# Where the scaling of the final norm's weights stands on ScalarE in the last feed-forward group

## The chip, the cores and the metric

The kernel runs on one NeuronCore of a Trainium2 chip. The metric is the device time of one execution in microseconds (us), as the median of several runs. All inputs lie in the chip's memory (HBM) at the start, and the output is written back there. Engines are called PE (TensorE matmuls), PEld (TensorE weight loads), DVE (VectorE), ACT (ScalarE), POOL (GpSimd) and SP (SyncE, which here only issues DMAs).

## What is computed

A trunk of two layers over 512 tokens of width 1024 in float32. Each layer has two groups of attention heads that share a projection, and then a dense feed-forward part with a squared ReLU. A final RMS norm with its own weights `final_norm` closes the trunk.

```python
def rmsnorm(x, g):
    return x * lax.rsqrt(jnp.mean(x * x, axis=-1, keepdims=True) + EPS) * g

for l in range(DEPTH):                                   # DEPTH = 2
    h = rmsnorm(x, attn_norm[l])
    ...                                                  # two kinds of attention, one output projection
    x = x + jnp.einsum('bse,ed->bsd', mixed, w_o[l])
    h = rmsnorm(x, mlp_norm[l])
    u = jnp.square(jax.nn.relu(jnp.einsum('bsd,df->bsf', h, w_ff1[l])))   # 1024 -> 4096
    x = x + jnp.einsum('bsf,fd->bsd', u, w_ff2[l])                        # 4096 -> 1024
return rmsnorm(x, final_norm)
```

## The kernel before

**Products in three matmuls.** Every float32 operand is split in a rounded part and a rest: for weights `whi` (rounded on ACT, L115) and `wlo` (the difference, made on DVE, L131). Each product is three matmuls (`three`, L297 with hi·hi, L298 with `wlo`, L299 with the activation's rest `Al`), which accumulate in one PSUM bank. Four pairs of buffers hold the split weights of the feed-forward part, used in turn: the rounding of a new tile waits until PE has done the last matmul with the tile four places earlier.

**Feed-forward groups.** The 4096 hidden columns are worked on in four groups (`GROUPS`). A group first makes its activations (`quad_group`, chains X, V, Y over `h`), and splits them into seven forms `Ah`, `Al` (L237 on ACT, L238 on DVE; the squared ReLUs stand in L1045 and L1046, sums of forms in L945). Then it multiplies the forms by seven sums of quarters of `w_ff2`, in the order `FORMS2`: "11", "x3", "21", "x2", "x1", "x4", "22". Each form has two weight tiles (called 0 and 1 below: x3/0, x3/1 and so on), and each tile serves twelve matmuls of 512 columns. The forms accumulate in three chains of two PSUM banks each: 11, x2, x1, 22 in X; x3, x4 in V; 21 in Y.

**Gathers.** After a form, `gather` (L1084) reads its two banks on DVE, scales them by the row factors and adds them to the result tiles `y`. Form x1 goes on accumulating in X, so its matmuls wait until the gather of x2 has read the banks.

**Weight sums by DMA.** `grow` (L861, L863) loads a quarter of `w_ff2` with SP or adds one to a tile in place with a POOL DMA. The adding load for x2 is issued as soon as the split of x3 has read the tile (x2/0 after x3/0, x2/1 after x3/1).

**End of the last group of the last layer.** Two DMAs of SP (L1245), written down after form x3, fetch `gfin` (the final norm's weights, to all 128 partitions) into `gf[0]` and `gf[1]`, which are pieces of `x`; they wait on SP for the last readers of these pieces. At form x2 three ACT instructions make the scaled weights: `gf[0]` by the root of D, `gf[1]` by minus that (L1247, L1248 of the profile), and `x[:, 0, 0:256]` from half of `gf[1]` (L1249). After form x1, four squares (`square`, L1107 on ACT) begin the sums for the last norm, and four `weigh` (L1145 on DVE) multiply finished pieces of `y` by `gf`. Form "22" and a chain of squares, roots (POOL, L1140), scalings and stores end the kernel.

**Order.** The program is written as one sequence; a scheduler that runs when the kernel is built, with a cost model of its own, places the instructions on each engine's queue by their dependencies and the order they were written in. An engine runs its queue strictly in that order. `behind(a, b)` adds an edge without a semaphore: `a` is placed after `b`. `in_order(a, b, c, ...)` chains such edges. `W.last[0]` is the newest rounding on ACT that has been written down when the line is reached; `W.do_split` writes them four tiles ahead of their use, so at form x2 the newest one is that of x4/0.

Of the kernel before, what the change touches and what calls it, by code (L numbers as in the profile page):

```python
# [12 lines left out]
AF = mybir.ActivationFunctionType  # L13
# [6 lines left out]
D = 1024  # L20
# [143 lines left out]
def trunk(ctx, tc, opened, xT, w, w2, w1, gfin, lamv, cos, sin, out):  # L164
    nc = tc.nc
# [19 lines left out]
    W = _Weights(nc, w, wraw, wspl)  # L185
# [3 lines left out]
    x = cp.tile([P, KC, S], F32, tag="x", name="x")  # L189
# [42 lines left out]
    r2 = cp.tile([P, 4], F32, tag="r2", name="r2")  # L232
# [27 lines left out]
    def behind(a, b):  # L260
        tc.add_manual_dep(a.ins, b.ins.name, mybir.DependencyInfo(
            mybir.DependencyClass.NoSync, mybir.DependencyReason.DATA), reason="order")
# [44 lines left out]
    def block(name, tag="mm"):  # L307
        pt = bank(tag, name)
        u = W.next("px" if name[0] == "p" else "1")
        for c in range(KC):  # L310
            three(pt, wpair(u, c), hpair(c), c == 0, c == KC - 1)
            yield pt if c == KC - 1 else None
# [20 lines left out]
    for l in range(L):  # L333
# [502 lines left out]
        with ExitStack() as fctx:  # L836
# [223 lines left out]
            def rest_of_forms(j, form):  # L1060
                F = [chunk(j, k) for k in range(4)]
                hi, lo = ([e[:, k, :, :].rearrange("p a t -> p (a t)") for k in range(7)] for e in sides[j])
                if form == "21":
                    split(hi[2], lo[2], F[3])
                elif form == "x2":
                    split_less(hi[5], lo[5], F[2])
                elif form == "22":
                    tt2(F[3], F[2], F[3], ALU.subtract)
                    split(hi[6], lo[6], F[3])
# [3 lines left out]
            def place(tb, j):  # L1073
                return y[(tb // 2, j)][:, tb % 2, :]
# [15 lines left out]
            def forth(tb, j):  # L1090
                pt = bank("t", f"xT{tb}{j}")
                for k in range(4):
                    nc.tensor.transpose(pt[:, k * P : (k + 1) * P], x[:, 4 * j + k, tb * P : (tb + 1) * P], ident)
                nc.scalar.activation(place(tb, j), pt, AF.Copy, scale=-1.0 if j else 1.0)
# [63 lines left out]
            def in_order(*steps):  # L1158
                for p, q in zip(steps[1:], steps):
                    behind(p, q)  # L1160

            gf = [x[:, 2, :], x[:, 3, :]]
# [5 lines left out]
            for g in range(GROUPS):  # L1168
                end = g == GROUPS - 1
                turn[0] = 0  # L1170
                if g:
                    p_, q_, r_, s_ = r_, s_, p_, q_
                    quad_group(g, 0, (p_, q_, r_))
                    quad_group(g, 1, (s_, r_, q_))
                    rest_of_forms(1, "21")
                else:
                    for k in range(2 * GP):
                        for n, pt in enumerate(block(f"f{l}_{g}_{k}", "any")):
                            if (k, n) == (1, 0):
                                rms_square(ssq, f"m{l}")  # L1180
                        evict_whole(pt, k)
                        h_form(k)
                        if last and k > 3:
                            for tb in (2 * (k % 2), 2 * (k % 2) + 1):
                                forth(tb, 1 - k // 6)
                    p_, q_, r_, s_ = ring[0] % 3, 3, (ring[0] + 1) % 3, (ring[0] + 2) % 3
                    held_on = {"Y": [bank("t", f"Y{l}{r}") for r in range(2)], "V": [bank("mm", f"V{l}{r}") for r in range(2)]}
                chains = {"X": [temp(k, f"X{l}{g}{k}") for k in (p_, q_)], **held_on}
                for form in FORMS2:
                    total, to = SUMS[form], chains[CHAIN[form]]  # L1190
                    opens = form == "11" or g == 0 and form in ("x3", "21")
                    if form == "x4" and not end:
                        to = [temp(k, f"W{l}{g}{k}") for k in (r_, s_)]
                        opens = True
                    work = [(c, i, r, 0) for c in range(GP // 2) for i in range(2) for r in range(2)]
                    tail = end and form == "22"
                    if tail and last:
                        gather(total, to)
                        to = [temp(k, f"Z{l}{k}") for k in (r_, s_)]
                        opens = True  # L1200
                        work = [(c, i, r, n) for r, n in ((0, 0), (1, 1), (1, 2)) for c in range(GP // 2) for i in range(2)]
                        halves = [to[1], bank("mm", "half")]
                        nc.tensor.matmul(
                            halves[1][:, 0:256], zeros[:, 0:128], zeros[:, 128:384], start=True, stop=False)
                        seed = nc.scalar.activation(
                            halves[1][:, 0:256], place(3, 1)[:, 256:512], AF.Copy, scale=mean[:, 3:4])
                    elif end and last and form == "x4":
                        work.sort(key=lambda e: e[2])
                    held = {}
                    for n, (c, i, r, part) in enumerate(work):  # L1210
                        if c not in held:
                            held[c] = W.next("f")
                        u = held[c]
                        hi, lo = (e[:, :, i, :] for e in sides[c])
                        rs = slice(r * P, r * P + P)
                        mine = [m for m, e in enumerate(work) if e[2:] == (r, part)]
                        pt, b_ = to[r], wpair(u, i, 512)
                        if part:
                            pt = halves[part - 1][:, 0:256]
                            b_ = [e[:, 256 * part - 256 : 256 * part] for e in b_]  # L1220
                        three(pt, (hi[:, SIDE[form], rs], lo[:, SIDE[form], rs]), b_,
                              opens and n == mine[0] and part < 2, n == mine[-1], not opens)
                        if tail and last and n == 3:
                            squares.append(square(0, 0))
                            first += [root(0), store(0, 0, False), came[1]]
                            squares += [seed, store(0, 1, True), square(1, 0)]
                            first += [root(1), store(1, 0, False), *gather(total, to, (0,))]
                            squares += [store(1, 1, True), square(2, 1)]
                            first.append(root(2))
                        if end and not last and form == "22" and n % 2:  # L1230
                            h = back(n // 2)
                            rests.append(h[1])
                            halfway = h
                    if tail:
                        break
                    if end or form not in ("x3", "21"):
                        came = gather(total, to)
                    if g and form in ("11", "x3"):
                        rest_of_forms(1, "x2" if form == "11" else "22")
                    if end and not last and form in ("21", "x2"):  # L1240
                        for c in range(4 * (form == "x2"), 4 * (form == "x2") + 4):
                            nc.sync.dma_start(x[:, c, :], park[c])
                    if end and last and form == "x3":
                        for c in range(2):
                            nc.sync.dma_start(gf[c], gfin[512 * c : 512 * c + 512].partition_broadcast(P))  # L1245
                    if end and last and form == "x2":
                        nc.scalar.activation(gf[0], gf[0], AF.Copy, scale=math.sqrt(D))  # L1247
                        nc.scalar.activation(gf[1], gf[1], AF.Copy, scale=-math.sqrt(D))  # L1248
                        nc.scalar.activation(x[:, 0, 0:256], gf[1][:, 256:512], AF.Copy, scale=r2[:, 3:4])  # L1249
                    if end and last and form == "x1":  # L1250
                        done = ((2, 0), (3, 0), (0, 1), (1, 1))
                        squares = [square(*e) for e in done]
                        weighed = [weigh(*e) for e in done]
                    elif end and last and form == "x4":
                        first = [came[0]]
# [94 lines left out]
```

## Time and profile before

| | us |
|---|---|
| median of 3 runs | 1139.09 |
| the runs | 1136.55, 1139.55, 1139.09 |
| profiled execution | 1138.57 |
| its span, first to last instruction | 1136.5 |
| PE busy in the span | 1122.4 (99%) |
| DVE busy | 914.9 (81%) |
| ACT busy | 687.0 (60%) |

The profiled execution takes 2.07 us outside its span. Times in the timeline are counted from the start of the span. In the timeline a row gives the start, the time an instruction takes, the engine, the line, out<-in with shapes, how many such instructions follow each other directly, and in brackets how long the engine had idled before it and what ended that idle time. The columns of the table by stretches of time stand in the order of the engines PE, PEld, DVE, ACT, POOL, then PEclk (granted TensorE clock, 1 is full), the busy share of the DMA engines, and GB/s. Matmuls are pipelined: one takes 0.39 us from start to end, and the next starts well before that.

### The profile page before, as it was taken

To read this page: it belongs to the slowest core of one execution; us is meant where nothing else is said; L and a number is where in the kernel's file an instruction comes from. 1 tells how busy PE (TensorE), PEld (TensorE's weight loads), DVE (VectorE), ACT (ScalarE), POOL (GpSimd) and SP (SyncE) were. 2 spreads that over 40 slices of the span, in tenths; PEclk is the share of its full clock that TensorE was granted. 3 is DMA by queue.
4 is the path that set the end of the run, shared out by engine and by line. 5 is a ranking of instruction groups with operands and counts; after the bars stand their busy time and mean duration, and the time that the engine had idled before them with its cause. 6 is when DMAs were issued, how large, how long until landed. Compare 5 with 4: busy or idle time off the path is not lost.

```text
span 1136.5 us, 17656 instructions
## 1 busy us (share of the span) xinstructions
PE 1122.4 (99%) x6613; PEld 992.6 (87%) x6613; DVE 914.9 (81%) x1329; ACT 687.0 (60%) x1115; POOL 137.5 (12%) x221
## 2 busy tenths in 40 slices
PE   9999999999999999999999999999999999999996
PEld 7899889888899899898888998988888998988975
DVE  7898788788669879779788877887877797797886
ACT  6456666567558457476345565675774574764763
POOL 1001343101001001001000014330010010010000
PEclk9999999999999999999999999999999999999998
DMA  7665353266877657738227544512487577567261
GB/s 250 149 187 147 93 168 112 74 207 161 234 195 165 173 163 168 204 110 224 75 78 206 162 131 130 159 65 75 167 198 199 159 167 204 149 154 216 78 128 75
DMA packets 59317, 174.99 MB, mean 154 GB/s; under 512 B 7264, under 2 KB 8544, under 8 KB 59232
## 3 DMA queue, kind: packets, MB, share of 16 engines
q1 hardware_dynamic: 50160, 141.84, 39.9%
q0 software_dynamic: 8640, 31.46, 15.8%
q8 instruction: 52, 0.85, 0.3%
q10 hardware_dynamic: 432, 0.56, 0.1%
q14 instruction: 33, 0.27, 0.1%
HBM read 144.47 MB, written 4.19 MB: 131 GB/s over the span
## 4 chain that ended last, share of the span: by engine, by line
PE 88%; DVE 5%; DMA 2%; issue 2%; ACT 1%; SPq 1%; POOL 0%; POOLq 0%; DVEq 0%; ACTq 0%
PE X L297 8%; PE X L298 8%; PE X L299 8%; PE V L297 3%; PE V L298 3%; PE V L299 3%; PE wo L297 3%; PE wo L299 3%; PE wo L298 3%; PE f L297 3%; PE f L299 3%; PE f L298 3%; PE Y L298 2%; PE Y L297 2%; PE Y L299 2%
## 5 line engine op out<-in xcount | busy, mean ns | idle before, releaser
L115 ACT ACTIVATE whi<-q 128x1024 fp32r<-128x1024 f32 x96 | 101.3, 1058 | 105.8 <-PE X L299 36.7
L131 DVE TENSOR_TENSOR wlo<-q,whi 128x1024 fp32r<-128x1024 f32 x96 | 116.9, 1221 | 42.2 <-ACT whi L115 39.1
L115 ACT ACTIVATE whi<-raw 128x1024 fp32r<-128x1024 f32 (+1 forms) x82 | 80.7, 992 | 49.6 <-issue 20.3
L131 DVE TENSOR_TENSOR wlo<-raw,whi 128x1024 fp32r<-128x1024 f32 (+1 forms) x82 | 95.2, 1168 | 10.9 <-ACT whi L115 10.5
L297 PE MATMUL X<-whi,Ah 128*128 128x512 f32 x248 | 98.2, 396 | 0.0
L298 PE MATMUL X<-wlo,Ah 128*128 128x512 f32 x248 | 97.1, 392 | 0.0
L299 PE MATMUL X<-whi,Al 128*128 128x512 f32 x248 | 96.9, 391 | 0.0
L131 DVE TENSOR_TENSOR wlo<-waves,whi 128x1024 fp32r<-128x1024 f32 x40 | 48.9, 1222 | 17.0 <-ACT whi L115 16.8
L115 ACT ACTIVATE whi<-waves 128x1024 fp32r<-128x1024 f32 x40 | 42.2, 1055 | 29.9 <-PE X L299 14.8
L297 PEld LDWEIGHTS X<-whi,Ah 128*128 128x128 f32 x248 | 46.9, 189 | 12.1 <-DVE y L1084 1.9
L299 PEld LDWEIGHTS X<-whi,Al 128*128 128x128 f32 x248 | 46.9, 189 | 10.0
L297 PE MATMUL X<-hxh,whi 128*128 128x256 f32 x192 | 54.9, 286 | 0.4 <-DVE x L1041 0.2
L298 PEld LDWEIGHTS X<-wlo,Ah 128*128 128x128 f32 x248 | 46.9, 189 | 9.0
L299 PE MATMUL X<-h_hi,wlo 128*128 128x256 f32 x192 | 54.4, 283 | 0.0
L298 PE MATMUL X<-h_lo,whi 128*128 128x256 f32 x192 | 54.4, 283 | 0.0
L298 PE MATMUL X<-hxl,whi 128*128 128x256 f32 x192 | 54.3, 283 | 0.0
L299 PE MATMUL X<-hxh,wlo 128*128 128x256 f32 x192 | 54.3, 283 | 0.0
L297 PE MATMUL X<-h_hi,whi 128*128 128x256 f32 x192 | 54.3, 283 | 0.0
L297 PE MATMUL f<-h_hi,whi 128*128 128x512 f32 x128 | 50.3, 393 | 0.0
L863 POOL DMA_DIRECT2D q<-in_w x32 | 28.7, 898 | 177.9 <-DVE wlo L131 177.9
L299 PE MATMUL f<-h_hi,wlo 128*128 128x512 f32 x128 | 49.9, 390 | 0.0
L298 PE MATMUL f<-h_lo,whi 128*128 128x512 f32 x128 | 49.8, 389 | 0.0
(740 smaller groups left out, 3819.1 us busy)
## 6 DMA issues: line engine op xcount, KB each, us to landing
raw<-in_w SPq DMA_DIRECT2D x78, 512.0 KB, 3.8
q<-in_w SPq DMA_DIRECT2D x48, 512.0 KB, 4.7
q<-in_w POOLq DMA_DIRECT2D x48, 512.0 KB, 7.5
waves<-in_w SPq DMA_DIRECT2D x28, 512.0 KB, 4.7
first_a<-in_w SPq DMA_DIRECT2D x12, 512.0 KB, 4.9
first_b<-in_w SPq DMA_DIRECT2D x12, 512.0 KB, 5.1
first_c<-in_w SPq DMA_DIRECT2D x12, 512.0 KB, 3.7
norms<-in_w SPq DMA_DIRECT2D x12, 512.0 KB, 3.6
```

Of the source, the lines that this page charges most:

```text
L115: return self.nc.scalar.activation(o, src, AF.Copy)
L131: self.last = h, nc.vector.tensor_tensor(out=lo[:, a:b], in0=raw[:, a:b], in1=hi[:, a:b].bitcast(F32), op=ALU.subtract)
L297: nc.tensor.matmul(pt, ah, bh, start=first, stop=False, skip_group_check=goes_on)
L298: nc.tensor.matmul(pt, ah, bl, start=False, stop=False, skip_group_check=goes_on)
L299: nc.tensor.matmul(pt, al, bh, start=False, stop=last, skip_group_check=goes_on)
L863: nc.gpsimd.dma_start(t, quad(g, q, c), accum_op=ALU.add)
```

## The change

The three ACT instructions that scale the final norm's weights are chained behind each other and behind the newest weight rounding on ACT.

```diff
                     if end and last and form == "x2":
-                        nc.scalar.activation(gf[0], gf[0], AF.Copy, scale=math.sqrt(D))
-                        nc.scalar.activation(gf[1], gf[1], AF.Copy, scale=-math.sqrt(D))
-                        nc.scalar.activation(x[:, 0, 0:256], gf[1][:, 256:512], AF.Copy, scale=r2[:, 3:4])
+                        in_order(
+                            W.last[0], nc.scalar.activation(gf[0], gf[0], AF.Copy, scale=math.sqrt(D)),
+                            nc.scalar.activation(gf[1], gf[1], AF.Copy, scale=-math.sqrt(D)),
+                            nc.scalar.activation(x[:, 0, 0:256], gf[1][:, 256:512], AF.Copy, scale=r2[:, 3:4]))
```

Later lines move down by one (L1247 to L1249 become L1248 to L1250). The queue of ACT, as the two programs were built, differs in this stretch; roundings are named by their weight tile, the right column is after the change:

```
before                               after
rounding x3/0                        rounding x3/0
L1045 relu                           L1045 relu
L1248 scale gf[1]                    L1046 square
L1046 square                         rounding x3/1
L1055 relu                           L237
L237                                 L1055 relu
L1056 square                         L237 (1024 columns)
L237 (1024 columns)                  L1056 square
L237                                 rounding 21/0
rounding x3/1                        L237
rounding 21/0                        L242
L242                                 rounding 21/1
rounding 21/1                        rounding x2/0
L1247 scale gf[0]                    rounding x2/1
rounding x2/0                        rounding x1/0
rounding x2/1                        L237
rounding x1/0                        rounding x1/1
L237                                 L1107 square
L1249 scale x[:, 0, 0:256]           rounding x4/0
rounding x1/1                        L1248 scale gf[0]
rounding x4/0                        L1249 scale gf[1]
L1107 square, twice                  L1107 square
rounding x4/1                        L1250 scale x[:, 0, 0:256]
rounding 22/0                        rounding x4/1
                                     rounding 22/0
```

On DVE the same instructions stand in the stretch: the split of x3/1 (`wlo`) moves forward by four places, that of 21/0 by one, and one `weigh` moves ahead of the split of x4/1. On PE one matmul of form x4 (L298) moves from ahead of the matmuls of x1 to behind them, and the matmul that prepares the last bank (L1203) moves ahead by one. The queues of POOL and SP keep their order.

## The prediction

> **What bounds the kernel now.** I read the page first, for the busy shares.
>
> ```profile
> PE 1122.4 (99%) x6613; PEld 992.6 (87%) x6613; DVE 914.9 (81%) x1329; ACT 687.0 (60%) x1115; POOL 137.5 (12%) x221
> ```
>
> PE sets the pace, so the change can gain only where PE stands still, or in the tail behind it. The edit touches a few microseconds in the last group. So the second view is the timeline of ACT there, with two rows of the preceding half group for comparison.
>
> ```profile
> 1062.37 1.06 ACT L1045 ACTIVATE x<-x 128x1024 f32<-128x1024 f32 x1 [0.95 <-DVE x L945]
> 1063.46 1.06 ACT L1046 ACTIVATE x<-x 128x1024 f32<-128x1024 f32 x1
> ...
> 1081.96 1.04 ACT L1045 ACTIVATE x<-x 128x1024 f32<-128x1024 f32 x1
> 1085.81 0.63 ACT L1248 ACTIVATE x<-x 128x512 f32<-128x512 f32 x1 [2.81 <-DMA x<-in_gfin]
> 1086.35 1.04 ACT L1046 ACTIVATE x<-x 128x1024 f32<-128x1024 f32 x1
> ```
>
> The scaling L1248 got between the ReLU and the square. It waits 2.81 us for the DMA of `gfin`, and the square L1046 waits behind it. In the half group before, L1046 starts 1.09 us after L1045, here 4.39 us. Who waits for the square is seen on DVE.
>
> ```profile
> 1082.09 1.23 DVE L131 TENSOR_TENSOR wlo<-q,whi 128x1024 fp32r<-128x1024 f32 x1 [0.28 <-ACT whi L115]
> 1087.42 1.42 DVE L945 TENSOR_TENSOR x<-x 128x512 f32<-128x512 f32 x2 [4.11 <-ACT x L1046]
> ...
> 1105.34 1.41 DVE L1084 SCALAR_TENSOR_TENSOR y<-Y,r,y 128x512 f32<-128x512 f32 x2
> 1106.66 2.36 DVE L131 TENSOR_TENSOR wlo<-q,whi 128x1024 fp32r<-128x1024 f32 x2
> 1108.93 1.41 DVE L1084 SCALAR_TENSOR_TENSOR y<-X,r,y 128x512 f32<-128x512 f32 x2
> ```
>
> DVE idles 4.11 us, and then never catches up, as the table by stretches shows: from 1087.42 to 1109.02, where the second `wlo` of the row at 1106.66 (that of x4/0) ends, it is busy for 21.53 of 21.60 us (third column).
>
> ```profile
> 1087.42:1109.02 21.60, 19.08 (x83) 15.13 (x81) 21.53 (x26) 15.26 (x22) 0.86 (x1) 1.00 0.48 109
> ```
>
> PE pays for that twice.
>
> ```profile
> 1091.98 0.39 PE L297 MATMUL V<-whi,Ah 128*128 128x512 f32 x1
> 1093.10 0.50 PE L298 MATMUL V<-wlo,Ah 128*128 128x512 f32 x1 [0.73 <-DVE wlo L131]
> 1093.44 0.39 PE L299 MATMUL V<-whi,Al 128*128 128x512 f32 x1
> ...
> 1106.61 0.61 PE L297 MATMUL V<-whi,Ah 128*128 128x512 f32 x2
> 1109.08 0.53 PE L298 MATMUL V<-wlo,Ah 128*128 128x512 f32 x1 [1.85 <-DVE wlo L131]
> 1109.42 0.61 PE L299 MATMUL V<-whi,Al 128*128 128x512 f32 x1
> ...
> 1112.82 0.40 PE L299 MATMUL X<-whi,Al 128*128 128x512 f32 x1
> 1113.06 0.39 PE L297 MATMUL X<-whi,Ah 128*128 128x512 f32 x1
> ...
> 1116.91 0.39 PE L299 MATMUL X<-whi,Al 128*128 128x512 f32 x1
> ```
>
> The first wait is for the `wlo` of x3/1, the second for that of x4/0. The granted clock (third value from the end) falls right after the second:
>
> ```profile
> 1105.00:1110.00 5.00, 3.15 (x13) 2.28 (x12) 5.00 (x7) 2.54 (x6) 0.00 (x0) 0.94 0.35 105
> 1110.00:1115.00 5.00, 5.00 (x18) 3.97 (x17) 2.68 (x4) 0.33 (x1) 0.00 (x0) 0.72 0.01 3
> 1115.00:1120.00 5.00, 5.00 (x24) 4.14 (x23) 4.24 (x5) 3.01 (x6) 0.00 (x0) 1.00 0.01 2
> ```
>
> Last, what the end hangs on: the rounding of 22/0 on ACT, and DVE behind it.
>
> ```profile
> 1114.67 1.06 ACT L115 ACTIVATE whi<-q 128x1024 fp32r<-128x1024 f32 x1 [6.21 <-issue]
> 1115.76 1.23 DVE L131 TENSOR_TENSOR wlo<-q,whi 128x1024 fp32r<-128x1024 f32 x1 [3.08 <-ACT whi L115]
> 1115.76:1122.60 6.84, 6.84 (x32) 5.50 (x31) 6.84 (x9) 2.83 (x7) 0.00 (x0) 1.00 0.00 0
> ```
>
> That rounding takes the buffers of x1/0, and so waits for the twelfth matmul of form x1 (second of the rows below, 1114.19 plus 0.39 is 1114.58). Behind it DVE works without a gap, and then DVE, ACT and POOL hand each other squares and roots to the end. So the end moves by as much as this twelfth matmul does.
>
> ```profile
> 1110.68 0.63 PE L297 MATMUL X<-whi,Ah 128*128 128x512 f32 x1
> 1114.19 0.39 PE L299 MATMUL X<-whi,Al 128*128 128x512 f32 x1
> ```
>
> **The change, part by part.** The pace of PE at full clock is 3.85 us for the 17 steps from 1113.06 to 1116.91, 0.2265 us each.
>
> *The square moves forward.* With no scaling ahead of it, L1046 starts 1.09 us after L1045, at 1083.05 instead of 1086.35: 3.30 us earlier. L945 starts 1.07 us behind the square, as now, so DVE takes up its work at 1084.12.
>
> *DVE keeps most of that lead.* Up to the `wlo` of x4/0 it has the same 26 instructions in another order, 21.60 us: that `wlo` would end at 1105.72 instead of 1109.02. What could hold DVE in between is PE or ACT. Y, the chain gathered before it, ends 72 steps after the group's first matmul (1083.80, below), at 1100.1, its gather comes at 1102.0. ACT's roundings wait for PE to free buffers, as now, and come before DVE needs them. I take the lead at x4/0 as 2.9 to 3.3 us, because ACT and DVE wait for each other in small pieces (0.35 us at one L237 below, and 0.07 in the next step).
>
> *The new wait.* x4/0's rounding now stands behind a square L1107, which waits for the first Y gather. That gather ends at 1105.34 + 0.75 − 3.30 = 1102.79, half of the 1.41 us row with the overlap. The square with its read takes 0.66 us (1106.13 to 1106.79), the rounding 1.04: 1104.5 to 1104.6. DVE reaches the split at 1105.72 − 1.23 = 1104.49. It costs at most 0.1. Behind the rounding now stand three scalings (0.63, 0.62 and 0.49 us below), another square and the rounding of x4/1. That tile is needed behind the 24 matmuls of x1, over 5 us later, so these cost nothing; without this cover they would cost their 1.7 us.
>
> ```profile
> 1083.80 0.40 PE L297 MATMUL X<-whi,Ah 128*128 128x512 f32 x1
> 1093.73 0.62 ACT L1247 ACTIVATE x<-x 128x512 f32<-128x512 f32 x1
> 1101.46 0.63 ACT L237 ACTIVATE Ah<-x 128x512 fp32r<-128x512 f32 x1 [0.35 <-DVE x L945]
> 1102.00 0.49 ACT L1249 ACTIVATE x<-x,r 128x256 f32<-128x256 f32 x1
> 1106.13 0.63 ACT L1107 ACTIVATE x<-y 128x512 f32<-128x512 f32 x1 [0.92 <-DVE y L1084]
> 1106.79 0.63 ACT L1107 ACTIVATE x<-y 128x512 f32<-128x512 f32 x1
> ```
>
> *PE's first wait goes.* The split of x3/1 moves ahead of four DVE instructions, and DVE is early. The rows show 1.12 and 0.34 us for two steps of 0.23: 1.00 us back.
>
> *PE's second wait goes, nearly.* From 1106.61 to the third matmul it takes 2.47 us instead of two steps (0.45), and then 0.34 for 0.23: 2.13 us back. PE, 1.00 earlier, wants the `wlo` of x4/0 at 1106.06. DVE has it at 1109.08 − 3.30 = 1105.78; PE stalls when DVE's lead falls below 3.02. With a lead of 2.9 it would stall 0.1. The gather of x2 then runs beside the other V matmuls; x1 needs it after five of these instead of six, so up to 0.2 more. I take 0.35 for the two, bounds 0 and 0.8 (a lead of 2.5, twice the small waits).
>
> *The slow clock goes with it.* From 1109.42 to 1112.82 eight steps take 3.40 us instead of 1.81: 1.59 us back. The idle time left, 0.1 to 0.4 us, is less than the 0.73 at 1093.10, after which the steps ran at full pace.
>
> *One V matmul moves behind x1*: 0.23 us sooner for the twelfth matmul of x1.
>
> Sum: 1.00 + 2.13 + 1.59 + 0.23 − 0.35 = 4.60 us. The profiled execution took 1138.57, so 1133.97, rounded **1134.0 us**. It lies 0.5 below the median of the three runs, which spread by 3.0; that spread goes into the range.
>
> A rule speaks against one term. The Trainium skill, page "TensorE: Matmul & The Clock Gate", section "Why this matters for your kernels", says that gaps of over some 3 us between bursts of matmuls bring the half clock, one window of idleness. The trace differs: 1.85 us were followed by it.
>
> **The rivals.**
>
> *The slow clock has another cause than this gap.* For: one case is thin evidence. Against: it begins 0.3 us after the gap. Then 1.59 stays: 1138.57 − 3.01 = 1135.6 us. By the skill's rule just named, this would be the outcome.
>
> *DVE's lead melts.* If ACT's new order (the rounding of x4/0 behind a square behind a gather) costs 1.2 us more than worked out, PE stalls for over 1 us there, and the slow clock comes again. Then the first wait, 1.00, the moved matmul, 0.23, and some 0.6 of the second are gained: 1136.7 us. For: DVE is busy to 99.7% there, and has only 0.28 us to spare. Against: the instructions are the same.
>
> *It does nothing to DVE*, because the square waits for something else: 1138.6 us. Against it: L1045 ended at 1083.0, and the square of the preceding half group followed its ReLU at once.
>
> *Slower: the adding load of x2/1 collides.* It is issued when the split of x3/1 has read the tile, and so moves from 1093.40 to about 1086.6, from an idle stretch of the DMA engines into a full one (1.04 and 0.16 in the rows).
>
> ```profile
> 1083.67 0.86 POOL L863 DMA_DIRECT2D q<-in_w x1 [1.88 <-DVE wlo L131]
> 1093.40 0.86 POOL L863 DMA_DIRECT2D q<-in_w x1 [8.87 <-DVE wlo L131]
> 1085.00:1090.00 5.00, 5.00 (x24) 4.14 (x23) 2.51 (x4) 4.19 (x7) 0.00 (x0) 1.00 1.04 230
> 1090.00:1095.00 5.00, 4.27 (x19) 3.23 (x18) 5.00 (x7) 5.00 (x7) 0.86 (x1) 1.00 0.16 28
> 1099.10 2.01 ACT L115 ACTIVATE whi<-q 128x1024 fp32r<-128x1024 f32 x2 [3.81 <-DVE y L1084]
> ```
>
> Now it takes 5.7 us until the rounding of x2/1 starts (1093.40 to 1099.10). Started only when the others are through, near 1091, it would be there at 1096.7; DVE wants the split at 1098.0, a rounding (1.06) before that is 1096.9. Past this point each us delays DVE, the Y gather, the square and x4/0 by one. Landing at 1105 would cost 8 us, make 1134.0 into 1142 us and bring the slow clock anyway. Against: the queue would have to stand for 8 us.
>
> **How the numbers follow.** Forecast, 1134.0: 0.70; its own range is 1132.0 (no residual stall, and runs 1.6 lower) to 1135.8. Slow clock stays, 1135.6: 0.09. Lead melts, 1136.7: 0.11. Nothing, 1138.6: 0.04. Slower, 1142: 0.06. The range 1132.0 to 1137.0 takes in the first three. A change of 0.3%, 3.4 us, is about what a measurement of this kernel can tell from none. Faster by more: the forecast and a little of the others, 0.73. Within: 0.21. Slower: 0.06.
>
> **What would show it.** In the changed profile L1046 follows L1045 by 1.1 us, DVE's idle time at L945 is below 1 us, both waits of PE for `wlo` in V are gone or below 0.4 us, the clock is 1.00 up to the tail, and the rounding of 22/0 starts near 1110. A wait of DVE for the rounding of x2/1 or x4/0 of over 0.5 us, or a clock below 1 between 1100 and 1115, would make the forecast wrong.

## The result, and the profile after

| | kernel before | changed kernel |
|---|---|---|
| median, runs side by side | 1138.67 us (6 runs, 1136.55 to 1140.04) | 1133.62 us (6 runs, 1132.63 to 1134.12) |
| profiled execution | 1138.57 us, span 1136.5 | 1134.11 us, span 1132.2 |
| first matmul of the last half group (the forms' products with `w_ff2`, from form "11" on) to the end of the span | 1136.5 − 1083.80 = 52.70 us | 1132.2 − 1084.47 = 47.73 us |

The ratio is 0.9957, with a 95% interval of 0.9944 to 0.9970: 5.05 us faster in the medians; 1134.0 us had been forecast. The third line of the table is used throughout below. The profiled executions of this kernel and its variants reach the last half group anywhere between 1082.25 and 1087.09 us, and this spread comes about ahead of the edit. Counted from that half group's first matmul (1083.80 before, 1084.47 after), only the stretch in which the edit acts is compared.

ACT around the ReLU (L1045) and the square (L1046), and then around the three scalings at their new place (L1248 to L1250, one line further down than before), in the timeline of the changed kernel:

```profile
1082.63 1.04 ACT L1045 ACTIVATE x<-x 128x1024 f32<-128x1024 f32 x1
1083.71 1.06 ACT L1046 ACTIVATE x<-x 128x1024 f32<-128x1024 f32 x1
...
1103.57 0.63 ACT L1107 ACTIVATE x<-y 128x512 f32<-128x512 f32 x1 [1.44 <-DVE y L1084]
1104.20 1.04 ACT L115 ACTIVATE whi<-q 128x1024 fp32r<-128x1024 f32 x1
1105.15 0.61 ACT L1248 ACTIVATE x<-x 128x512 f32<-128x512 f32 x1
1105.67 0.61 ACT L1249 ACTIVATE x<-x 128x512 f32<-128x512 f32 x1
...
1110.37 1.06 ACT L115 ACTIVATE whi<-q 128x1024 fp32r<-128x1024 f32 x1 [2.12 <-PE X L299]
```

The square follows the ReLU by 1.08 us; before it was 4.39. The scalings wait for nothing 22 us later. The last row is the rounding of 22/0, on which the tail hangs: it starts 4.30 us sooner than the one at 1114.67 before. DVE:

```profile
1084.80 1.42 DVE L945 TENSOR_TENSOR x<-x 128x512 f32<-128x512 f32 x2 [0.81 <-ACT x L1046]
...
1104.11 2.39 DVE L131 TENSOR_TENSOR wlo<-q,whi 128x1024 fp32r<-128x1024 f32 x2
1106.42 1.40 DVE L1084 SCALAR_TENSOR_TENSOR y<-X,r,y 128x512 f32<-128x512 f32 x2
```

Its idle time for the square has shrunk from 4.11 to 0.81 us, and the two splits that ended near 1109.02 now end at 1106.50. PE, from the half group's first matmul, over the V matmuls of x4/0, to the first and the twelfth matmul of x1:

```profile
1084.47 0.40 PE L297 MATMUL X<-whi,Ah 128*128 128x512 f32 x1
...
1106.25 0.62 PE L297 MATMUL V<-whi,Ah 128*128 128x512 f32 x2
1106.71 0.39 PE L298 MATMUL V<-wlo,Ah 128*128 128x512 f32 x1
...
1107.40 0.39 PE L297 MATMUL X<-whi,Ah 128*128 128x512 f32 x1
...
1109.95 0.39 PE L299 MATMUL X<-whi,Al 128*128 128x512 f32 x1
```

No row has a wait any more. The matmul that waited 1.85 us for its `wlo` starts one ordinary step after its predecessor, and the twelfth matmul of x1 comes 25.48 us after the half group's first, before 30.39: 4.91 us less. In the stretches, PE is busy throughout and the granted clock (third value from the end) is 1.00:

```profile
1105.00:1110.00 5.00, 5.00 (x24) 4.05 (x23) 5.00 (x7) 3.25 (x7) 0.00 (x0) 1.00 0.02 5
1110.00:1115.00 5.00, 5.00 (x24) 4.14 (x23) 3.69 (x6) 2.97 (x5) 0.00 (x0) 1.00 0.00 0
```

### The profile page after: what moved, and what is told of

Same layout as the page of the kernel before. It is cut to its first block, busy times and chain, and to the rows that moved or that the text cites. A ratio compares the mean times of both kernels' runs of the same rounds, so it can differ in the third digit from the quotient of the medians.

```text
span 1132.2 us, 17656 instructions
## 1 busy us (share of the span) xinstructions
PE 1119.7 (99%) x6613; PEld 990.9 (88%) x6613; DVE 915.6 (81%) x1329; ACT 687.8 (61%) x1115; POOL 137.6 (12%) x221
## 4 chain that ended last, share of the span: by engine, by line
PE 94%; DVE 2%; DMA 1%; issue 1%; ACT 1%; POOL 0%; POOLq 0%; DVEq 0%; ACTq 0%
PE X L297 9%; PE X L298 9%; PE X L299 9%; PE V L297 3%; PE V L299 3%; PE V L298 3%; PE wo L297 3%; PE wo L299 3%; PE wo L298 3%; PE f L297 3%; PE f L299 3%; PE f L298 3%; PE Y L297 2%; PE Y L299 2%; PE Y L298 2%; DMA first_b<-in_w 1%
## 5 line engine op out<-in xcount | busy, mean ns | idle before, releaser
L298 PE MATMUL X<-wlo,Ah 128*128 128x512 f32 x248 | 96.7, 390 | 0.0
L298 PEld LDWEIGHTS X<-wlo,Ah 128*128 128x128 f32 x248 | 46.6, 188 | 8.9
L298 PE MATMUL X<-h_lo,whi 128*128 128x256 f32 x192 | 54.3, 283 | 0.0
L298 PE MATMUL X<-hxl,whi 128*128 128x256 f32 x192 | 54.3, 283 | 0.0
L298 PE MATMUL f<-h_lo,whi 128*128 128x512 f32 x128 | 49.8, 389 | 0.0
```

Source lines behind the costliest of these rows:

```text
L298: nc.tensor.matmul(pt, ah, bl, start=False, stop=False, skip_group_check=goes_on)
```

## The experiments

The theory: the wait for the load of `gf[1]`, in front of the square, is what costs the time, by way of DVE's lead and PE's two waits, and PE's idle time then brings the half clock (a granted clock of 0.50). The main rivals: it is not the wait but the new order of the queues, or the half clock has another cause. The scaling of `gf[1]` alone, the short load and the two loads in pieces ran on one chip (kernel before: 1136.96 us, 23 runs), the other eight kernels on another (1136.71 us in 31 runs of the kernel before beside `gf[0]` alone, the kernel without the load and the first two of the half clock; 1136.87 us in 14 beside the last four). Below, the anchor is the rounding behind which a kernel chains its scalings.

### One scaling at a time

Only the scalings of `gf[1]` behind the anchor, and then only that of `gf[0]`:

```diff
+ in_order(W.last[0], nc.scalar.activation(gf[1], gf[1], AF.Copy, scale=-math.sqrt(D)))   # e1
...
+ in_order(W.last[0], nc.scalar.activation(gf[0], gf[0], AF.Copy, scale=math.sqrt(D)))    # e2
```

> The kernel before, with only the scaling of gf[1] chained behind the rounding of x4/0; that of gf[0] is left free and stands now ahead of L242, behind the rounding of 21/0. Theory: the place of gf[1]'s scaling is all that matters for the square, so the gain is that of the whole change, 1133.6 us; a new wait of up to 1 us for gf[0]'s load may show at its new place and cost up to 0.8 us (1134.4). Rival (the three together, or their chaining, are needed): 1136 us or more.

> Only the scaling of gf[0] is ordered behind the newest weight rounding; those of gf[1] stay free. Theory: the scaling that stands between the ReLU and the square is that of gf[1], and stays there; it waits 2.5 to 3 us for its load, PE waits 0.7 to 0.8 and 1.8 to 1.9 us for wlo as before, and the time is within 0.1% of the kernel before. Rival (the anchored scalings gain by their number or by room on ACT later): a third of the gain, 1.5 us, is there.

With `gf[1]` alone: 1133.24 us, ratio 0.9968 (0.9956 to 0.9980), 47.97 us from the half group's start to the end, as good as the whole change. With `gf[0]` alone: 1136.21 us, ratio 0.9991 (0.9983 to 1.0000), 51.38 us, and the old picture, here ACT and PE of that kernel:

```profile
1085.03 0.63 ACT L1248 ACTIVATE x<-x 128x512 f32<-128x512 f32 x1 [3.00 <-DMA x<-in_gfin]
...
1092.32 0.50 PE L298 MATMUL V<-wlo,Ah 128*128 128x512 f32 x1 [0.92 <-DVE wlo L131]
1108.29 0.50 PE L298 MATMUL V<-wlo,Ah 128*128 128x512 f32 x1 [1.83 <-DVE wlo L131]
```

So the scaling between ReLU and square is nearly the whole matter: it leaves 0.24 us of the 4.97 to the other two. With `gf[1]` alone, ACT still stands before a scaling, that of `gf[0]`, at another place:

```profile
1092.70 0.63 ACT L1247 ACTIVATE x<-x 128x512 f32<-128x512 f32 x1 [1.98 <-DMA x<-in_gfin]
```

The trace puts 1.98 us of idle time down to the load there, and no wait of PE follows. The same stall on the same engine costs at most those 0.24 us where nobody is about to need what is queued behind it.

### The wait without the order, and a shorter and a slower load

Is it the wait or the order? In the first kernel here the load of `gf[1]` is left out, and its scaling is held where the kernel before has it. In the second only 64 of each 512 weights are loaded. The third fetches the same bytes in reversed pieces of 64, and the fourth does so in the changed kernel. The cuts below stand one behind the other.

```diff
- for c in range(2):                                             # e7: gf[0] only
+ for c in range(1):
...
+ s1 = nc.scalar.activation(gf[1], gf[1], AF.Copy, scale=-math.sqrt(D))
+ in_order(W.relu, s1, W.sq)
...
+ nc.sync.dma_start(gf[c][:, 0:64], gfin[512 * c : 512 * c + 64].partition_broadcast(P))   # e5
...
+ nc.sync.dma_start(gf[c].rearrange("p (a b) -> p a b", b=64)[:, ::-1, :],                 # e6, a6
+     gfin[512 * c : 512 * c + 512].rearrange("(a b) -> a b", b=64)[::-1, :].partition_broadcast(P))
```

> This kernel is the kernel before with the scaling of gf[1] held by hand between the ReLU L1045 and the square L1046, where the kernel before has it, and with the load of gf[1] left out (the scaling works on what stood in its place, so the second half of the final norm's weights is not there). Every engine's queue holds the same instructions in the same order as in the kernel before, one load fewer on SP. Theory (the wait for the load costs the time, the place alone only the scaling's own 0.54 us): the scaling waits for nothing, the square starts about 1.6 us behind the ReLU, the two waits of PE for wlo (0.73 and 1.85 us) are gone or under 0.3 us together, no stretch with a granted clock under 0.97 between 1105 and 1115, and the time is 3 to 5 us under that of the kernel before. Rival (the new order of ACT, DVE and PE behind the anchor brings the gain, not the load's wait): the order is the old one, so the time stays within 1 us of the kernel before and PE's wait at the second half group's V matmul stays near 1.8 us.

> The kernel before, with only the first 64 of 512 columns of each half of gfin loaded (the other columns of the output are scaled by stale numbers); the queues of all engines are those of before, instruction by instruction. Theory (the wait of L1248 for the load): the load lands sooner, L1248 waits under 1 us instead of 2.8, the square comes 2.3 to 2.8 us sooner, both waits of PE for a wlo shrink to 0.5 us or less, the clock stays at 1.00, and the time is 4.2 us below before, near 1134.5 us when before is 1138.7. Rival (the new order of splits and matmuls does the work, not the wait): nothing changes, 1138.7 us. Rival (any instruction between ReLU and square costs it): also near before, PE still waits over 1.5 us.

> The kernel before, with each half of gfin loaded in eight pieces of 64 columns in reversed order, so that the load takes longer; same result, and the queues of all engines are those of before. Theory: L1248 waits d us longer than 2.8 us, the square, DVE and the second wait of PE move by the same d, and the time is before plus d, up to 1.7 us more if a second stretch of slow clock comes: with d of 1 to 4, 1140 to 1144 us. Rival (order does the work): 1138.7 us.

> The changed kernel with the same slower load. Theory: the scalings come some 20 us after the load, so its duration is hidden: 1133.6 us within 0.6, the square 1.1 us behind the ReLU, no wait of PE. Rival (the load itself, by its share of the DMA engines, delays the adding loads for x2, and that was what cost time): slower than the changed kernel by 1 us or more, and DVE waits for a rounding of x2.

The kernel without the load: 1134.15 us, ratio 0.9975 (0.9964 to 0.9985), 48.33 us from the half group's start to the end. ACT, DVE and PE of it:

```profile
1082.13 1.04 ACT L1045 ACTIVATE x<-x 128x1024 f32<-128x1024 f32 x1
1083.08 0.62 ACT L1248 ACTIVATE x<-x 128x512 f32<-128x512 f32 x1
1083.60 1.04 ACT L1046 ACTIVATE x<-x 128x1024 f32<-128x1024 f32 x1
...
1084.68 1.42 DVE L945 TENSOR_TENSOR x<-x 128x512 f32<-128x512 f32 x2 [1.19 <-ACT x L1046]
...
1105.76 0.61 PE L297 MATMUL V<-whi,Ah 128*128 128x512 f32 x2
1106.32 0.50 PE L298 MATMUL V<-wlo,Ah 128*128 128x512 f32 x1
1106.66 0.40 PE L299 MATMUL V<-whi,Al 128*128 128x512 f32 x1
```

Every queue has the order of before, the scaling stands where it stood, and PE's waits are gone but for some 0.2 us in the steps at 1106.32 and 1106.66. In the profiled executions that is 4.37 of the 4.97 us by which the changed kernel is shorter; the last 0.60 is what the scaling's place and the old order cost without a wait. As the main cause, the rival, the order, falls: the order of before with the load's wait taken out brings most of the gain. How small its share is stays open. In the medians the kernel without the load gains 2.56 us, and the changed kernel, run again below, 3.92, so 1.36 us lie between them; the intervals of the two ratios overlap (0.9964 to 0.9985, and 0.9958 to 0.9978).

The short load and the load in pieces went otherwise than expected. The short load brings 1135.45 us, ratio 0.9983 (0.9974 to 0.9992). It lands little sooner: the scaling's wait is 2.06 us instead of 2.81. The 0.75 us less was enough for PE's first wait, not for the second:

```profile
1085.35 0.63 ACT L1248 ACTIVATE x<-x 128x512 f32<-128x512 f32 x1 [2.06 <-DMA x<-in_gfin]
...
1108.61 0.50 PE L298 MATMUL V<-wlo,Ah 128*128 128x512 f32 x1 [1.86 <-DVE wlo L131]
```

The load in pieces was hardly later: a wait of 2.92 us, PE's waits 0.84 and 1.83, 1137.21 us, ratio 0.9998 (0.9989 to 1.0006). The two loads, of which that of `gf[1]` goes first, took 6.3 and 9.0 us from issue to landing in the kernel before, 5.5 and 6.1 with 64 weights, 6.4 and 10.0 in pieces. So size and pieces hardly decide when `gf[1]` lands, though they do move `gf[0]`, and these kernels say little on how much a longer wait costs. In the changed kernel the load in pieces gave 1133.00 us, ratio 0.9968 (0.9955 to 0.9981), 47.71 us from the half group's start to the end. That is as expected, but with a load that is hardly slower it tests little.

### The half clock

The load in pieces showed something else: the same idle time of PE, 1.83 us, and no half clock behind it. Three kernels test this. In all of them x4's matmuls are ordered behind x1's, so that PE's idle time lies in one piece ahead of x1; the second fills it with matmuls of zeros, the third lengthens it by six copies on DVE.

```diff
+ behind(W.head, W.x1) if end and last and form == "x4" else setattr(W, "x1", W.mm)    # all three
...
+ for _ in range(13 if end and last and form == "x2" else 0):                          # f13
+     behind(nc.tensor.matmul(held_on["V"][0], zeros[:, 0:128], zeros[:, 128:640], start=False, stop=False, skip_group_check=True), W.mm)
...
+ for n_ in range(6 if end and last and form == "x2" else 0):                          # f0_long
+     nc.vector.tensor_copy(h_hi[:, 0, 0:512], to[n_ % 2])
```

> The kernel before, with the matmuls of form x4 ordered behind those of x1 on PE, so that PE stands idle between the last matmul of x2 and the first of x1, which waits for the gather on DVE, about 3 us in one piece instead of 1.85 us. No fillers. Theory (an idle PE brings the half clock): the granted clock falls below 0.8 in the 5 us behind the gap, the twelfth matmul of x1 starts about 1113.9, within 0.5 us of the kernel before (1114.19). Rival (the half clock there has another cause, such as the load on the chip at that moment, and the gap does not matter): the clock in this kernel and in the one with 13 fillers is the same, and the times of both differ by less than 0.5 us.

> As the kernel without fillers, with 13 matmuls of zeros (128 by 512, added to bank 0 of V, which changes nothing in it) put right behind the last matmul of x2: at 0.23 us each they fill the 3 us in which PE would stand idle. Theory (an idle PE brings the half clock): the granted clock stays at 1.00 through 1105 to 1115, the twelfth matmul of x1 starts about 1112.3, and the time is 1.2 to 1.9 us under that of the kernel without fillers. Rival (another cause): the clock falls here too, and the times agree within 0.5 us.

> The kernel with x4's matmuls behind x1's and no fillers, with six copies of X by DVE (128 by 512 each, about 0.7 us) put into its queue behind the gather that frees X, so that PE's idle time ahead of x1 grows from 3.04 us to 5 or more. Only the granted clock behind the gap is of interest, not the time. Theory (the half clock follows from idle time of PE, but not in each execution while the gap is short): behind a gap of over 5 us the clock falls in the profiled execution, by about 1.7 us in the sum of the two stretches behind it, and the mean granted clock is 0.996 or less in each run. Rival (idle time of PE has nothing to do with it): clocks of 0.997 to 0.998 in most runs, and 1.00 behind the gap in the profiled execution.

Without fillers: 1137.67 us, ratio 1.0003 (0.9992 to 1.0013). With them: 1136.23 us, ratio 0.9995 (0.9986 to 1.0003). The medians stand 1.44 us apart, inside the 1.2 to 1.9 expected, but the two intervals overlap, so the times do not settle it. The mean granted clock that is on record for every run says more: without fillers it is 0.996 or less in six of twelve runs (median 1138.0 us; the other six 1135.8), with fillers in none of eleven. But the profiled execution without fillers has its 3.04 us of idle time and no half clock at all: there the expectation was wrong. With six copies PE waits 8.48 us ahead of x1 (1144.60 us, ratio 1.0064), and the half clock is there, in each run by the mean clock of 0.993.

What decides in the profiled executions is seen when the windows view is cut not at round numbers but at the moments where the clock changes. In the kernel before it falls at 1109.42 and comes back at 1112.83, 3.41 us later, and falls again in the tail, where PE is done, at 1129.89: 20.47 us after the first time, six times 3.41. Columns as above, length and busy time of PE first:

```profile
1106.00:1109.42 3.42, 1.57 (x8) 0.98 (x6) 3.42 (x5) 2.33 (x5) 0.00 (x0) 1.00 0.32 131
1109.42:1112.83 3.41, 3.41 (x10) 2.64 (x9) 3.26 (x5) 0.00 (x0) 0.00 (x0) 0.50 0.02 5
...
1126.48:1129.89 3.41, 0.63 (x6) 0.42 (x4) 2.02 (x4) 1.51 (x4) 0.82 (x2) 1.00 0.46 176
1129.89:1133.30 3.41, 0.00 (x0) 0.00 (x0) 1.82 (x5) 2.23 (x6) 0.61 (x2) 0.50 0.36 141
```

So the clock is set in slots of 3.41 us on a fixed grid, and in the slots ahead of these two half ones PE is idle for 1.85 and 2.78 us. The tail gives the grid of the other executions too (their clock falls at 1128.52 without fillers, at 1128.88 with the load in pieces). Counted back by it, first the kernel without fillers:

```profile
1104.63:1108.04 3.41, 1.93 (x9) 1.27 (x7) 3.41 (x5) 2.51 (x6) 0.00 (x0) 1.00 0.48 154
1108.04:1111.45 3.41, 1.84 (x8) 1.57 (x9) 3.41 (x5) 0.19 (x1) 0.00 (x0) 1.00 0.02 5
1111.45:1114.86 3.41, 3.41 (x17) 2.81 (x16) 2.08 (x3) 1.06 (x1) 0.00 (x0) 1.00 0.01 2
```

then the load in pieces:

```profile
1104.98:1108.40 3.42, 2.44 (x11) 1.69 (x9) 3.42 (x5) 2.52 (x6) 0.00 (x0) 1.00 0.52 153
1108.40:1111.81 3.41, 2.56 (x11) 2.15 (x12) 3.41 (x5) 0.23 (x1) 0.00 (x0) 1.00 0.02 5
```

and the long gap, where the clock's own changes give the grid:

```profile
1107.48:1110.89 3.41, 0.46 (x3) 0.03 (x1) 3.41 (x5) 2.12 (x5) 0.00 (x0) 1.00 0.22 89
1110.89:1114.30 3.41, 0.00 (x0) 0.00 (x0) 3.41 (x6) 0.00 (x0) 0.00 (x0) 0.50 0.00 0
1114.30:1117.71 3.41, 1.29 (x3) 0.96 (x4) 3.19 (x5) 0.00 (x0) 0.00 (x0) 0.50 0.02 5
1117.71:1121.12 3.41, 3.41 (x9) 2.73 (x9) 0.00 (x0) 0.00 (x0) 0.00 (x0) 0.50 0.00 0
1121.12:1124.54 3.42, 3.42 (x16) 2.78 (x16) 1.76 (x2) 1.21 (x2) 0.00 (x0) 1.00 0.01 2
```

The 3.04 us without fillers happened to lie across a boundary, 1.48 in one slot and 1.57 in the next, and the clock stayed. The 1.83 us of the load in pieces was cut into 0.98 and 0.85. In the kernel before, the wait lay in one slot. In the long gap a slot at half clock with 1.29 us of work (2.12 idle) is followed by another at half clock, and a fully busy one by the full clock. A slot in which PE stands for 1.57 us does nothing, one with 1.85 us halves the next. The tail of the changed kernel's second profile, cut by its own grid, narrows this: 1.68 us idle, and the next slot still has the full clock.

```profile
1122.36:1125.77 3.41, 1.73 (x15) 1.53 (x13) 1.63 (x4) 1.67 (x5) 0.56 (x1) 1.00 0.50 192
1125.77:1129.18 3.41, 0.00 (x0) 0.00 (x0) 2.12 (x7) 2.15 (x6) 1.08 (x2) 1.00 0.32 125
```

Two more executions fit: the short load (1.86 us within one slot, half clock) and `gf[0]` alone (cut into 1.07 and 0.76, none). Over their whole length, no slot of the fourteen profiled executions speaks against it. The Trainium skill, "TensorE: Matmul & The Clock Gate", section "What's actually happening", describes such a window: 3413 ns long and free-running. The 3.41 us and the six times 3.41 agree with it. This reading was made after the runs; none was made to put a gap at a chosen place of the grid. That the place of a gap decides is therefore shown by these profiles alone; that idle time of PE brings the half clock is also shown by the fillers and the long gap.

### What the new place costs

The kernel before with the scalings left out (the final norm's weights go in unscaled), then with the scalings behind an earlier rounding, and the changed kernel again beside them:

```diff
- nc.scalar.activation(gf[0], gf[0], AF.Copy, scale=math.sqrt(D))      # e3: all three out
...
+ anchor = W.last[0]                                                   # e4: taken at form x3
+ in_order(anchor, nc.scalar.activation(gf[0], gf[0], AF.Copy, scale=math.sqrt(D)),
```

> The kernel before with the three scalings of the final norm's weights left out; the loads stay, the weights of the final norm go in unscaled. Theory (behind the anchor the scalings cost nothing, as ACT has room there): the same time as the changed kernel, within 0.5 us; from the first matmul of the group's second half to the end of the span 47.5 to 48 us (47.7 in the changed kernel, 52.7 in the kernel before), no wait of PE between 1083 and 1113. Rival (the scalings behind the anchor still cost their 0.52, 0.52 and 0.41 us, as the work queued behind them on ACT is on the way to the end): 1 to 1.5 us under the changed kernel.

> The changed kernel with its three scalings ordered behind an earlier weight rounding, that of the first weights of x2 instead of that of the first weights of x4, about 11 us earlier on ACT and 7 us behind the landing of gf[1]'s load. Theory (only where the scaling waits for its load does it cost; any place behind the landing will do): the same time as the changed kernel within 0.6 us, no wait for the load, no wait of PE over 0.3 us. Rival (the late anchor itself matters, since ACT in between is needed by DVE): a wait for wlo is back on PE, and the time is 1 to 2 us over that of the changed kernel.

> The changed kernel once more, beside the others on one chip. Theory (the place between ReLU and square costs its own 0.54 us on DVE's lead and hardly anything on PE, the load's wait costs the rest): from the first matmul of the group's second half to the end of the span 47.7 us, 0.6 us under the kernel without gf[1]'s load (48.3), and 3.2 to 4.2 us under the kernel before in the medians. Rival (the new order is worth as much as the wait): 1.5 us or more under the kernel without gf[1]'s load against the same kernel before, which stood 2.6 us under it.

| | median | ratio to before | half group's start to the end |
|---|---|---|---|
| no scalings | 1133.53 us | 0.9972 (0.9960 to 0.9984) | 47.85 us |
| earlier anchor | 1132.66 us | 0.9960 (0.9947 to 0.9972) | 47.81 us |
| changed kernel again | 1132.95 us | 0.9968 (0.9958 to 0.9978) | 47.73 us |

The three cannot be told apart. The scalings cost nothing that can be seen behind the anchor, and the anchor need not be late: with the earlier one the scalings of `gf[0]` and `gf[1]` (L1249 and L1250 of that kernel) follow a rounding without a wait. What counts is that the scaling of `gf[1]` stands behind the landing of its load and not ahead of the square.

```profile
1092.35 0.61 ACT L1249 ACTIVATE x<-x 128x512 f32<-128x512 f32 x1
1092.87 0.62 ACT L1250 ACTIVATE x<-x 128x512 f32<-128x512 f32 x1
```

None of these kernels beats the changed one by more than the intervals.

## Why the prediction was right, and where it was not

- **The square moves forward.** Forecast 1.09 us behind the ReLU, measured 1.08.
- **DVE keeps its lead.** Forecast 2.9 to 3.3 us at the `wlo` of x4/0. Against its own ReLU it ends at 1106.50 − 1082.63 = 23.87 us, before 1109.02 − 1081.96 = 27.06: a lead of 3.19.
- **The new wait.** At most 0.1 us was allowed for x4/0's rounding behind the square L1107. It ends at 1105.24, and DVE's two splits run through without a wait: nothing.
- **PE's waits.** Both gone. The residual of 0.35 us was the mis-sized term: PE wanted the `wlo` at 1106.71, DVE had it at 1106.50, and x1 follows the fifth V matmul at once. Measured: none.
- **The moved V matmul.** As forecast, five instead of six ahead of x1.
- **The sum.** Without the residual it was 1.00 + 2.13 + 1.59 + 0.23 = 4.95 us; measured 4.91 at the twelfth matmul of x1 and 4.97 at the end. The profiled execution was already 0.67 us late when it reached the half group, which makes the spans differ by 4.3.
- **The slow clock.** The term was right for the execution that was costed and is too large as a mean. The idle time does bring the half clock, but only where enough of it falls into one slot. In the profiled executions with the wait of 1.83 to 1.86 us it came in two of four. Without it the half group takes 51.24 or 51.38 us instead of 52.70, so it costs some 1.4 us when it comes. From slots of 3.41 us and a bound between 1.68 and 1.85, a gap of 1.85 us has a chance of 46% to 56% to bring it (an estimate, if it falls anywhere on the grid alike: (3.41 − 1.85 + 2 × 0 to 0.17) / 3.41). So the typical gain is 3.5 to 3.7 us of removed waiting plus about half of 1.4. The first comparison gave 5.05, the repeat 3.92. The mean clock of the timed runs points the same way: of the 68 runs of the kernel before beside the experiments, 21 have 0.996 or less, as the two profiled ones with this half clock do, with a median of 1137.9 us; the other 47 have 1136.7, and none of the 15 runs of the changed kernel lies below 0.997. That the clock made the difference between the two comparisons is not shown: the first has no clock on record for its timed runs of the kernel before.
- **Luck in the number.** The forecast was counted down from 1138.57 us, one execution with the half clock. The 68 later runs of the kernel before have a median of 1136.9 us, and from there the same 4.60 us would have led to 1132.3, against 1132.95 in the repeat. Why the first six runs stood 1.7 us higher stays open. So the steps were right, and that the time came out within 0.4 us is in part luck.
- **The rule that was weighed.** It is that of the Trainium skill, "TensorE: Matmul & The Clock Gate", section "Why this matters for your kernels", against gaps of over some 3 us. It fails both ways here: 1.85 us brought the half clock and 3.04 us did not. The prediction was right to let the trace decide, and wrong to take one execution for all of them.
- **The rivals.** The lead did not melt. The adding load of x2/1 did move forward, to 1087.71, and collided with nothing: the rounding of its tile waits for PE, not for the load.

```profile
1087.71 0.86 POOL L863 DMA_DIRECT2D q<-in_w  x1 [2.51 <-DVE wlo L131]
...
1095.57 1.06 ACT L115 ACTIVATE whi<-q 128x1024 fp32r<-128x1024 f32 x1 [1.66 <-PE V L299]
```

## What to carry to other kernels

On an in-order queue a small instruction that waits for a load delays what stands behind it, so look for waits on loads ahead of work that feeds the busiest engine, and order them behind something that comes after the landing; two such places cost the same here. To cost such a wait, follow it to the engine that sets the pace: 2.81 us on ACT, with the scaling's own 0.54, became 3.30 us on DVE (4.11 of idle time against 0.81), about 3.1 us on PE, and now and then 1.4 us more by the clock. Compare profiles from a common mark just ahead of the edit, because the profiled executions here differed by up to 4.8 us before they reached it.

## What the runs showed of the hardware

The granted clock changes on a grid of 3.41 us that does not start with the kernel (it falls at 1109.42 us in the kernel before and at 1110.89 with the long gap, 1.47 us apart), so whether an idle stretch of 1.8 to 3 us halves the clock is a matter of where it falls: 1.85 us in one slot did, 3.04 us cut into 1.48 and 1.57 did not. The first of two loads took 5.5 us from issue to landing with 64 weights per row and 6.3 with 512, the second 6.1 and 9.0. Neither had been expected.
